# Two transformer blocks in split fp32r: the order of the three products per weight unit when the tokens are stationary

## The chip, the cores and the metric

The kernel runs on one core of one Trainium2 chip, as one program for the whole network. The metric is device time in microseconds (us) of one execution; three executions of the kernel before gave a median of 2867.14 us (2867.01 to 2867.37). The trace that is read here is of another, profiled execution, which took 2861.25 us.

## The reference

256 tokens of width 1024 go through two stacked blocks of two layers each. In the first block a layer is a hybrid mixer (three kinds of attention), a cross-attention to a memory, and a feed-forward part: a dense SwiGLU in layer 0, a mixture of 8 experts with the best 2 per token in layer 1. In the second block a layer is SwiGLU, another hybrid mixer, SwiGLU. Nearly all work is matrix products of fp32 activations with fp32 weights that are read once:

```python
def swiglu(t, w_gu, w_down):
    a, g = jnp.split(t @ w_gu, 2, axis=-1)
    return (jax.nn.silu(a) * g) @ w_down

def moe_swiglu(h, w_router, w_gu, w_down):
    ...
    gate = jnp.einsum('tk,tke->te', top_w, jax.nn.one_hot(top_idx, N_EXPERTS, ...))
    out = jnp.zeros_like(t)
    for e in range(N_EXPERTS):
        out = out + gate[:, e:e + 1] * swiglu(t, w_gu[e], w_down[e])
```

## The kernel before, in words

A product of two fp32 matrices is made of three products in the fp32r format. Each operand is split into a high part (`hi`, the value cast to fp32r) and a low part (`lo`, what the cast left over), and hi times hi, hi times lo and lo times hi are added up in the same PSUM tile; lo times lo is left out.

Weights come from HBM in units of 512 KB: `load_raw` (L156) starts the DMA into a tile `raw`, and `split_raw` (L162) has the scalar engine (ACT) cast it to `hi` (L167) and the vector engine (DVE) take `lo` = `raw` - `hi` (L169). There are 8 buffers each of `raw`, `hi` and `lo`. A unit is 128 partitions by 1024 columns: two row blocks of 128 weight rows with 512 columns (or four with 256, or one with 1024).

"Tokens stationary" means that a 128 by 128 piece of the split activations is loaded into TensorE and a row block of weights streams past it, 512 columns per matmul. `mm3` (L179) issues the three matmuls of one row block: tokens hi by weights hi (L181), tokens hi by weights lo (L182), tokens lo by weights hi (L183). In a row of the trace the first name behind the arrow is the streamed weight part and the second (T, G or Z) the stationary tile, so "mm<-lo,T" is the product with the low part of the weights, and its LDWEIGHTS row is the load of the stationary part for it. `projs` (L188) calls it for every row block of a projection, `proj_steps` (L208) and `merge` do the same in pieces, `proj_acc` (L257) runs the dense down projections with both halves of the columns and both token halves, and `expert` (L962) the down projection of an expert.

The experts take up the middle of the program, from about 862 to 1652 us. Tokens of an expert are gathered into one set of 128 slots. Its 2816 hidden columns come in five chunks of 512 and one of 256. Of a chunk `projs` computes the a half and then the g half, four units each (here a0 to a3 and g0 to g3). Six matmuls a unit make 48 matmuls. When a is complete, ACT takes its tanh (L975), and DVE multiplies it on (L802). When g is complete, DVE multiplies again (L803), four transposes on TensorE (L296, tile `pT`) turn the result, ACT casts it (L285) and DVE takes its low part (L286). After the six chunks two down projections of 11 units each follow, whose result is split (L285 and L286, tile `y`) and scattered back (L1015).

Each engine runs its instructions in a fixed order that is set when the program is built. The order is found by a scheduler of the framework that goes by its own estimates of when operands are ready; the cast and the low part of a unit get a priority 30 places ahead of their turn (`high_priority(offset=self.lead)`), and a low part may be held behind a chain of norm operations (`behind_chain`). So a change in the order of the matmuls can change where, on ACT and DVE, the casts and low parts of units stand against L975, L802, L803 and L286.

The few lines that matter most:

```python
def mm3(self, ps, a, b, first, last):                 # L179, before
    mm(ps, a[0], b[0], start=first, stop=False)       # L181 tokens hi, weights hi
    mm(ps, a[0], b[1], start=False, stop=False)       # L182 tokens hi, weights lo
    mm(ps, a[1], b[0], start=False, stop=last)        # L183 tokens lo, weights hi
```

Of the kernel before, what the change touches and what calls it, by code (L numbers as in the profile page):

```python
# [20 lines left out]
P = 128  # L21
D = 1024
S = 256
KC = D // P
DEPTH = 2
DFF = 2816
FC = DFF // P
# [32 lines left out]
class _Net:  # L60
# [48 lines left out]
    def mm(self):  # L109
        return self.pmm.tile([P, 512], F32, tag="mm", name="mm")  # L110
# [61 lines left out]
    def behind_chain(self):  # L172
# [3 lines left out]
        self.ahead += 1  # L176
        return self.tc.issue_after(self.chain[0 if self.ahead <= self.upto else -1][1])

    def mm3(self, ps, a, b, first, last):  # L179
        mm = self.nc.tensor.matmul  # L180
        mm(ps, a[0], b[0], start=first, stop=False)  # L181
        mm(ps, a[0], b[1], start=False, stop=False)  # L182
        mm(ps, a[1], b[0], start=False, stop=last)  # L183
# [4 lines left out]
    def projs(self, X, jobs, toks=2):  # L188

        work = []  # L190
        self.upto = AHEAD * len(jobs)
        for W, pieces, evac in jobs:
            n = sum(b - a for a, b in pieces)
            per = 2 if n > 256 else 4
            work.append((n, per, evac, [
                self.unit(*[W[k * P:(k + per) * P, a:b].rearrange("(k p) n -> p k n", p=P) for a, b in pieces])
                for k in range(0, KC, per)]))
        self.upto = AHEAD
        for t in range(toks):
            for n, per, evac, units in work:  # L200
                ps = self.mm()[:, :n]
                for k in range(KC):
                    u = units[k // per]
                    self.mm3(ps, (X[0][:, k, t * P:(t + 1) * P], X[1][:, k, t * P:(t + 1) * P]),
                             (u[0][:, k % per], u[1][:, k % per]), k == 0, k == KC - 1)
                evac(t, ps)

    def proj_steps(self, X, W, c0, evac):  # L208

        units = []  # L210

        def step(t):
            if t == 0:
                units.extend(self.unit(W[k * P:(k + 2) * P, c0:c0 + 512].rearrange("(k p) n -> p k n", p=P))
                             for k in range(0, KC, 2))
            ps = self.mm()
            for k in range(KC):
                u = units[k // 2]
                self.mm3(ps, (X[0][:, k, t * P:(t + 1) * P], X[1][:, k, t * P:(t + 1) * P]),
                         (u[0][:, k % 2], u[1][:, k % 2]), k == 0, k == KC - 1)  # L220
            evac(t, ps)
        return [lambda: step(0), lambda: step(1)]

# [33 lines left out]
    def proj_acc(self, lhs, W, kc, fin):  # L257
        tail = min(TAIL, kc)
        self.chain, self.ahead = [], 0
        both = self.ps_s()  # L260
        acc = [[both[:, 0], both[:, 1]], [self.mm(), self.mm()]]

        def step(u, k, t):
            a = lhs(k, t)
            for half in range(2):
                cs = slice(half * 512, (half + 1) * 512)
                self.mm3(acc[t][half], a, (u[0][:, 0, cs], u[1][:, 0, cs]), k == 0, k == kc - 1)

        def get(k):
            return self.unit(W[k * P:(k + 1) * P].rearrange("(k p) n -> p k n", p=P))  # L270

        for k in range(kc - tail):
            u = get(k)
            for t in range(2):
                step(u, k, t)
        us = [get(k) for k in range(kc - tail, kc)]
        for t in range(2):
            for j, u in enumerate(us):
                step(u, kc - tail + j, t)
            fin(t, acc[t])  # L280
# [431 lines left out]
    def merge(self, Y, branches, gates):  # L712

        nc = self.nc
        self.lead = LEAD
        M = self.new_x()
        for c in range(2):
            cs = slice(512 * c, 512 * c + 512)
            units = [[self.unit(w[k * P:(k + 2) * P, cs].rearrange("(k p) n -> p k n", p=P))
                      for k in range(0, w.shape[0] // P, 2)] for _, w, _ in branches]  # L720
            for t in range(2):
                tok = slice(t * P, (t + 1) * P)
                m = None
                for us, (gi, w, k0) in zip(units, branches):
                    ps = self.mm()
                    n = 2 * len(us)
                    for k in range(n):
                        u = us[k // 2]
                        self.mm3(ps, (Y[0][:, k0 + k, tok], Y[1][:, k0 + k, tok]), (u[0][:, k % 2], u[1][:, k % 2]),
                                 k == 0, k == n - 1)  # L730
                    x = self.ptile()[:, :512]
                    nc.vector.scalar_tensor_tensor(x, gates[:, t, gi * D + 512 * c:gi * D + 512 * c + 512], 1.0, ps,
                                                   ALU.add, ALU.mult)
                    if m is not None:
                        nc.vector.tensor_add(x, x, m)
                    m = x
                sl = (slice(None), slice(4 * c, 4 * c + 4), tok)
                self.transpose_split([m[:, j * P:(j + 1) * P] for j in range(4)], M[0][sl], M[1][sl], 0.5)
        return M
# [222 lines left out]
    def expert(self, e, X, back, gate, mids, more, rows):  # L962
# [3 lines left out]
        hi, lo = (a[:, o:o + FC * P].rearrange("p (k s) -> p k s", k=FC) for a in mids)  # L966
        wgu = d["moe_w_gu"][0, e]
        wd = d["moe_w_down"][0, e]
        for c0, c1 in FF_CHUNKS:
            n = c1 - c0  # L970
# [19 lines left out]
        for hf in range(2):  # L990
            cs = slice(hf * 512, (hf + 1) * 512)
            ps = self.mm()
            for k in range(0, FC, 2):
                u = self.unit(wd[k * P:(k + 2) * P, cs].rearrange("(k p) n -> p k n", p=P))
                for j in range(2):
                    self.mm3(ps, (hi[:, k + j], lo[:, k + j]), (u[0][:, j], u[1][:, j]), k + j == 0, k + j == FC - 1)
            if rows and hf:
                rows = rows()
            sums = self.scatter(e, hf, ps, y, back, gate, hf and rows, sums if hf else None)
# [489 lines left out]
```

## Time and profile before

| what | value |
|---|---|
| median of three runs | 2867.14 us (2867.01 to 2867.37) |
| the profiled execution | 2861.25 us, its span in the trace 2859.5 us |
[...]
| TensorE (PE) busy with matmuls | 2785.7 us, 97% |
| loads of stationary parts (PEld) | 2295.5 us, 80% |
| DVE busy | 2186.8 us, 76% |
| ACT busy | 1653.3 us, 58% |
| moved by DMA | 632.97 MB, 221 GB/s in the mean |

How to read it: all engines work at once, each on its own list of instructions, and an instruction waits for its operands with everything behind it on that engine. A busy PE is no PE at its peak, since a matmul's row also covers time in which the next one already streams; what counts is how far apart the matmuls start. In rows of the timeline, "x3" joins three instructions that follow one another, and the brackets give the idle time ahead of a row and what ended it. Waits of an engine that has time to spare cost nothing by themselves.

### The profile page before, as it was taken

The page shows a single profiled execution, that of the slowest core. Times are in us where ns is not written, and L with a number is a line of the kernel's source. Part 1 is how long each engine was busy: PE and PEld are TensorE (multiplying, and loading weights), DVE is VectorE, ACT ScalarE, POOL GpSimd, SP SyncE. Part 2 cuts the span into 40 slices and gives each one's busy share as a digit, 9 for nine tenths or more (in the row PEclk, how much of TensorE's full clock was granted, in tenths as well). Part 3 has the DMA queues.
Part 4 walks back from the last instruction along what each step waited for, and adds up shares of the span by engine and source line. Part 5 has one row for each costly group of instructions (what it writes and reads, how often), then busy time and mean ns, then how long its engine had stood idle before and what let it go on. Part 6 is the DMA issues. An engine that isn't in the chain of part 4 may idle for free.

```text
span 2859.5 us, 39765 instructions
## 1 busy us (share of the span) xinstructions
PE 2785.7 (97%) x14147; PEld 2295.5 (80%) x14147; DVE 2186.8 (76%) x3635; ACT 1653.3 (58%) x2372; POOL 74.0 (3%) x134
## 2 busy tenths in 40 slices
PE   7999999999979999999999989999999999999999
PEld 6779888877967887788778768877788888777887
DVE  7766675777658899999989987597787575887774
ACT  5544454555447677777777756455455454555553
POOL 0100000010000000000000000001000000010000
PEclk9999999999989999999999989999999999999999
DMA  8546466554638999999999976555466566454563
GB/s 268 153 147 206 142 206 190 179 156 137 207 96 311 333 330 359 351 337 361 347 339 356 357 234 191 153 185 161 150 214 193 166 206 192 154 162 154 185 190 99
DMA packets 385583, 632.97 MB, mean 221 GB/s; under 512 B 33888, under 2 KB 171872, under 8 KB 385376
## 3 DMA queue, kind: packets, MB, share of 16 engines
q1 hardware_dynamic: 385376, 630.35, 67.3%
q8 instruction: 113, 1.85, 0.3%
q14 instruction: 94, 0.77, 0.1%
HBM read 629.22 MB, written 1.05 MB: 220 GB/s over the span
## 4 chain that ended last, share of the span: by engine, by line
PE 60%; DVE 7%; issue 1%; ACT 1%; DMA 0%; SPq 0%; ACTq 0%
PE mm L182 13%; PE mm L181 12%; PE mm L183 12%; PE mm L252 9%; PE mm L253 5%; DVE lo L169 2%; PE pS L182 2%; PE pS L181 2%; PE pS L183 2%; PE pT L296 2%; DVE sm L319 0%; PE pT L950 0%; DVE Z L1251 0%; DVE sm L1250 0%; DVE p L1115 0%
## 5 line engine op out<-in xcount | busy, mean ns | idle before, releaser
L169 DVE TENSOR_TENSOR lo<-raw,hi 128x1024 fp32r<-128x1024 f32 (+2 forms) x1170 | 1394.1, 1218 | 312.1 <-ACT hi L167 304.1
L167 ACT CAST hi<-raw 128x1024 fp32r<-128x1024 f32 (+2 forms) x1170 | 1189.6, 1048 | 416.1 <-PE mm L183 260.4
L182 PE MATMUL mm<-lo,T 128*128 128x512 f32 (+3 forms) x1868 | 728.8, 390 | 3.3 <-DVE sm L339 1.8
L181 PE MATMUL mm<-hi,T 128*128 128x512 f32 (+3 forms) x1868 | 719.9, 386 | 8.0 <-PEq L914 5.1
L183 PE MATMUL mm<-hi,T 128*128 128x512 f32 (+3 forms) x1868 | 715.4, 383 | 0.0
L252 PE MATMUL mm<-T,hi 128*128 128x512 f32 x1440 | 500.0, 393 | 0.0
L182 PEld LDWEIGHTS mm<-lo,T 128*128 128x128 f32 x1868 | 353.5, 189 | 90.8 <-DVE lo L169 28.7
L181 PEld LDWEIGHTS mm<-hi,T 128*128 128x128 f32 x1868 | 353.5, 189 | 82.9 <-issue 7.3
L183 PEld LDWEIGHTS mm<-hi,T 128*128 128x128 f32 x1868 | 353.7, 189 | 61.3 <-issue 1.4
L253 PE MATMUL mm<-T,lo 128*128 128x256 f32 x1440 | 400.8, 278 | 0.0
L252 PEld LDWEIGHTS mm<-T,hi 128*128 128x128 f32 x1440 | 269.7, 187 | 61.0
L253 PEld LDWEIGHTS mm<-T,lo 128*128 128x128 f32 x1440 | 271.1, 188 | 0.2
L182 PE MATMUL mm<-lo,G 128*128 128x512 f32 x636 | 249.1, 392 | 0.0
L181 PE MATMUL mm<-hi,G 128*128 128x512 f32 x636 | 248.2, 390 | 0.0
L183 PE MATMUL mm<-hi,Z 128*128 128x512 f32 x572 | 223.4, 390 | 0.0
L182 PEld LDWEIGHTS mm<-lo,G 128*128 128x128 f32 x636 | 119.4, 188 | 25.9 <-DVE lo L169 2.1
L429 POOL TENSOR_SCALAR p<-p,sm 128x256 f32<-128x256 f32 (+1 forms) x128 | 73.3, 585 | 2541.2 <-DVE sm L404 1662.7
L181 PEld LDWEIGHTS mm<-hi,G 128*128 128x128 f32 x636 | 119.5, 188 | 24.4
L183 PEld LDWEIGHTS mm<-hi,Z 128*128 128x128 f32 x572 | 107.4, 188 | 21.6
L285 ACT CAST T<-pT 128x512 fp32r<-128x512 f32 (+3 forms) x112 | 58.0, 521 | 103.3 <-PE pT L296 48.3
L286 DVE TENSOR_TENSOR T<-pT,T 128x512 fp32r<-128x512 f32 (+3 forms) x112 | 67.1, 608 | 50.3 <-ACT T L285 49.8
L254 ACT COPY q<-mm 128x256 f32<-128x256 f32 x180 | 65.6, 364 | 66.3 <-PE mm L253 66.3
(291 smaller groups left out, 2871.7 us busy)
## 6 DMA issues: line engine op xcount, KB each, us to landing
raw<-in_moe_w_gu_dram SPq DMA_DIRECT2D x352, 512.0 KB, 5.4
raw<-in_moe_w_down_dram SPq DMA_DIRECT2D x176, 512.0 KB, 5.8
raw<-in_w_in_dram SPq DMA_DIRECT2D x164, 512.0 KB, 4.5
raw<-in_ffn_w_down_dram SPq DMA_DIRECT2D x110, 512.0 KB, 4.1
raw<-in_ffn_w_gate_dram SPq DMA_DIRECT2D x88, 512.0 KB, 4.6
raw<-in_ffn_w_up_dram SPq DMA_DIRECT2D x88, 512.0 KB, 4.7
raw<-in_ffn_w_gu_dram SPq DMA_DIRECT2D x44, 512.0 KB, 4.7
raw<-in_w_out_dram SPq DMA_DIRECT2D x32, 512.0 KB, 4.1
```

Of the source, the lines that this page charges most:

```text
L167: nc.scalar.copy(hi, raw)
L169: nc.vector.tensor_sub(lo, raw, hi.bitcast(F32))
L181: mm(ps, a[0], b[0], start=first, stop=False)
L182: mm(ps, a[0], b[1], start=False, stop=False)
L183: mm(ps, a[1], b[0], start=False, stop=last)
L252: mm(ps, u[0][:, kk, cs], X[2][:, :, k], start=k == 0, stop=False)
L253: mm(ps[:, 0], u[1][:, kk, cs], X[0][:, k], start=False, stop=k == KC - 1)
L254: nc.scalar.copy(low[:, j], ps[:, 1])
L285: a = nc.scalar.copy(hi, ps)
L286: b = nc.vector.tensor_sub(lo, ps, hi.bitcast(F32))
L296: self.nc.tensor.transpose(ps[:, j * P:(j + 1) * P], s, self.ident)
L429: self.nc.gpsimd.tensor_scalar(dst[:, s], dst[:, s], rc[:, t:t + 1], 1.0, ALU.mult, ALU.mult)
```

## The change

A new helper `mm3x` takes all row blocks of one unit at once. It issues, for each row block, tokens hi by weights hi and tokens lo by weights hi, and after these, for each row block, tokens hi by weights lo. It replaces `mm3` in `projs`, `proj_steps`, the merge of the mixer and the down projection of an expert; in `proj_acc`, whose unit is one row block with two column halves, the same order is written out over the halves. The places where the weights are stationary (`proj_t`, `proj_f`), the router, the mixer's small products and the overflow path stay as they are. Every engine has as many instructions as before.

```diff
--- before.py
+++ after.py
@@ -176,6 +176,16 @@
         self.ahead += 1
         return self.tc.issue_after(self.chain[0 if self.ahead <= self.upto else -1][1])
 
+    def mm3x(self, ps, xs, ws, first, last):
+
+
+        mm = self.nc.tensor.matmul
+        for i, (x, w) in enumerate(zip(xs, ws)):
+            mm(ps, x[0], w[0], start=first and i == 0, stop=False)
+            mm(ps, x[1], w[0], start=False, stop=False)
+        for i, (x, w) in enumerate(zip(xs, ws)):
+            mm(ps, x[0], w[1], start=False, stop=last and i + 1 == len(xs))
+
     def mm3(self, ps, a, b, first, last):
         mm = self.nc.tensor.matmul
         mm(ps, a[0], b[0], start=first, stop=False)
@@ -199,10 +209,10 @@
         for t in range(toks):
             for n, per, evac, units in work:
                 ps = self.mm()[:, :n]
-                for k in range(KC):
-                    u = units[k // per]
-                    self.mm3(ps, (X[0][:, k, t * P:(t + 1) * P], X[1][:, k, t * P:(t + 1) * P]),
-                             (u[0][:, k % per], u[1][:, k % per]), k == 0, k == KC - 1)
+                tok = slice(t * P, (t + 1) * P)
+                for k, u in zip(range(0, KC, per), units):
+                    self.mm3x(ps, [(X[0][:, j, tok], X[1][:, j, tok]) for j in range(k, k + per)],
+                              [(u[0][:, j], u[1][:, j]) for j in range(per)], k == 0, k + per == KC)
                 evac(t, ps)
 
     def proj_steps(self, X, W, c0, evac):
@@ -214,10 +224,10 @@
                 units.extend(self.unit(W[k * P:(k + 2) * P, c0:c0 + 512].rearrange("(k p) n -> p k n", p=P))
                              for k in range(0, KC, 2))
             ps = self.mm()
-            for k in range(KC):
-                u = units[k // 2]
-                self.mm3(ps, (X[0][:, k, t * P:(t + 1) * P], X[1][:, k, t * P:(t + 1) * P]),
-                         (u[0][:, k % 2], u[1][:, k % 2]), k == 0, k == KC - 1)
+            tok = slice(t * P, (t + 1) * P)
+            for k, u in zip(range(0, KC, 2), units):
+                self.mm3x(ps, [(X[0][:, j, tok], X[1][:, j, tok]) for j in (k, k + 1)],
+                          [(u[0][:, j], u[1][:, j]) for j in range(2)], k == 0, k + 2 == KC)
             evac(t, ps)
         return [lambda: step(0), lambda: step(1)]
 
@@ -262,9 +272,13 @@
 
         def step(u, k, t):
             a = lhs(k, t)
-            for half in range(2):
-                cs = slice(half * 512, (half + 1) * 512)
-                self.mm3(acc[t][half], a, (u[0][:, 0, cs], u[1][:, 0, cs]), k == 0, k == kc - 1)
+            mm = self.nc.tensor.matmul
+            cuts = list(zip(acc[t], (slice(0, 512), slice(512, D))))
+            for ps, cs in cuts:
+                mm(ps, a[0], u[0][:, 0, cs], start=k == 0, stop=False)
+                mm(ps, a[1], u[0][:, 0, cs], start=False, stop=False)
+            for ps, cs in cuts:
+                mm(ps, a[0], u[1][:, 0, cs], start=False, stop=k == kc - 1)
 
         def get(k):
             return self.unit(W[k * P:(k + 1) * P].rearrange("(k p) n -> p k n", p=P))
@@ -724,10 +738,9 @@
                 for us, (gi, w, k0) in zip(units, branches):
                     ps = self.mm()
                     n = 2 * len(us)
-                    for k in range(n):
-                        u = us[k // 2]
-                        self.mm3(ps, (Y[0][:, k0 + k, tok], Y[1][:, k0 + k, tok]), (u[0][:, k % 2], u[1][:, k % 2]),
-                                 k == 0, k == n - 1)
+                    for k, u in zip(range(0, n, 2), us):
+                        self.mm3x(ps, [(Y[0][:, k0 + j, tok], Y[1][:, k0 + j, tok]) for j in (k, k + 1)],
+                                  [(u[0][:, j], u[1][:, j]) for j in range(2)], k == 0, k + 2 == n)
                     x = self.ptile()[:, :512]
                     nc.vector.scalar_tensor_tensor(x, gates[:, t, gi * D + 512 * c:gi * D + 512 * c + 512], 1.0, ps,
                                                    ALU.add, ALU.mult)
@@ -992,8 +1005,8 @@
             ps = self.mm()
             for k in range(0, FC, 2):
                 u = self.unit(wd[k * P:(k + 2) * P, cs].rearrange("(k p) n -> p k n", p=P))
-                for j in range(2):
-                    self.mm3(ps, (hi[:, k + j], lo[:, k + j]), (u[0][:, j], u[1][:, j]), k + j == 0, k + j == FC - 1)
+                self.mm3x(ps, [(hi[:, j], lo[:, j]) for j in (k, k + 1)], [(u[0][:, j], u[1][:, j]) for j in range(2)],
+                          k == 0, k + 2 == FC)
             if rows and hf:
                 rows = rows()
             sums = self.scatter(e, hf, ps, y, back, gate, hf and rows, sums if hf else None)
```

The build finds new places for some casts and low parts. Line numbers after the change are 13 or 14 higher: L802 is L815, L803 is L816, L975 is L988, L286 is L300, L343 is L357, and L184, L185, L187 are hi by hi, tokens lo by weights hi, and weights lo.

The first place is the second chunk of the third expert on DVE; its tanh is the L975 at 1076.71 us in the trace before. Here mm_21404 is the a half of a chunk, mm_21455 its g half; lo_21401 belongs to a3, lo_21434, 21440, 21446 and 21452 to g0 to g3, and lo_21493 to a0 of the next chunk. Before:

```order
L286 TENSOR_TENSOR Z_7985<-pT_21373,G_7984 128x512
L169 TENSOR_TENSOR lo_21401<-raw_21398,hi_21400 128x1024
L169 TENSOR_TENSOR lo_21434<-raw_21431,hi_21433 128x1024
L169 TENSOR_TENSOR lo_21440<-raw_21437,hi_21439 128x1024
L802 SCALAR_TENSOR_TENSOR p_21429<-p_21429,mm_21404 128x512
L169 TENSOR_TENSOR lo_21446<-raw_21443,hi_21445 128x1024
L169 TENSOR_TENSOR lo_21452<-raw_21449,hi_21451 128x1024
L169 TENSOR_TENSOR lo_21493<-raw_21490,hi_21492 128x1024
L803 SCALAR_TENSOR_TENSOR p_21480<-p_21429,mm_21455 128x512
```

After, on the same engine and at the same place:

```order
L300 TENSOR_TENSOR Z_7985<-pT_21373,G_7984 128x512
L169 TENSOR_TENSOR lo_21401<-raw_21398,hi_21400 128x1024
L169 TENSOR_TENSOR lo_21434<-raw_21431,hi_21433 128x1024
L815 SCALAR_TENSOR_TENSOR p_21429<-p_21429,mm_21404 128x512
L169 TENSOR_TENSOR lo_21440<-raw_21437,hi_21439 128x1024
L169 TENSOR_TENSOR lo_21446<-raw_21443,hi_21445 128x1024
L169 TENSOR_TENSOR lo_21452<-raw_21449,hi_21451 128x1024
L169 TENSOR_TENSOR lo_21493<-raw_21490,hi_21492 128x1024
L816 SCALAR_TENSOR_TENSOR p_21480<-p_21429,mm_21455 128x512
```

The multiplication by the a half (L802, now L815) has moved one low part earlier, so that the low part of g1 stands behind it. The same holds for 27 of the 40 chunks of 512 columns: the second to fifth chunk of experts 2, 4 and 6 (counted from 0), and all five of experts 3, 5 and 7.

On ACT at the same place, before:

```order
L285 CAST G_7984<-pT_21373 128x512
L167 CAST hi_21400<-raw_21398 128x1024
L167 CAST hi_21433<-raw_21431 128x1024
L167 CAST hi_21439<-raw_21437 128x1024
L975 ACTIVATE p_21429<-mm_21404 128x512
L167 CAST hi_21445<-raw_21443 128x1024
```

And after:

```order
L299 CAST G_7984<-pT_21373 128x512
L167 CAST hi_21400<-raw_21398 128x1024
L167 CAST hi_21433<-raw_21431 128x1024
L988 ACTIVATE p_21429<-mm_21404 128x512
L167 CAST hi_21439<-raw_21437 128x1024
L167 CAST hi_21445<-raw_21443 128x1024
```

The tanh (L975, now L988) has moved ahead of the cast of g1 in the same way. On PE the four transposes of a chunk's result come after a1's first matmul, where they came after four of a0's six.

The third place is the start of the dense feed-forward part of the first layer on DVE, at about 341 us: p_3297 and p_3324 are the first token half's products (L802 and L803), the sm tiles belong to the norm of the second token half, and h_88 is its result. Before:

```order
L802 SCALAR_TENSOR_TENSOR p_3297<-p_3297,mm_3272 128x512
L319 SCALAR_TENSOR_TENSOR sm_3189<-sm_3190,sm_3189 128x1
L315 SCALAR_TENSOR_TENSOR sm_3190<-sm_3189,sm_3191 128x1
L319 SCALAR_TENSOR_TENSOR sm_3189<-sm_3190,sm_3189 128x1
L315 SCALAR_TENSOR_TENSOR sm_3190<-sm_3189,sm_3191 128x1
L319 SCALAR_TENSOR_TENSOR sm_3189<-sm_3190,sm_3189 128x1
L343 SCALAR_TENSOR_TENSOR h_88<-h_88,sm_3189,gb_2978 128x512 x2
L803 SCALAR_TENSOR_TENSOR p_3324<-p_3297,mm_3299 128x512
```

After:

```order
L815 SCALAR_TENSOR_TENSOR p_3297<-p_3297,mm_3272 128x512
L329 SCALAR_TENSOR_TENSOR sm_3190<-sm_3189,sm_3191 128x1
L333 SCALAR_TENSOR_TENSOR sm_3189<-sm_3190,sm_3189 128x1
L329 SCALAR_TENSOR_TENSOR sm_3190<-sm_3189,sm_3191 128x1
L816 SCALAR_TENSOR_TENSOR p_3324<-p_3297,mm_3299 128x512
L333 SCALAR_TENSOR_TENSOR sm_3189<-sm_3190,sm_3189 128x1
L329 SCALAR_TENSOR_TENSOR sm_3190<-sm_3189,sm_3191 128x1
L333 SCALAR_TENSOR_TENSOR sm_3189<-sm_3190,sm_3189 128x1
L357 SCALAR_TENSOR_TENSOR h_88<-h_88,sm_3189,gb_2978 128x512 x2
```

The second product (L803, now L816) has moved ahead of the last steps of the norm of the second token half.

## Rows read from the trace of the kernel before

**Rows 1.** The page: busy times, and loads of stationary parts by line.

```profile
PE 2785.7 (97%) x14147; PEld 2295.5 (80%) x14147; DVE 2186.8 (76%) x3635; ACT 1653.3 (58%) x2372; POOL 74.0 (3%) x134
...
L182 PEld LDWEIGHTS mm<-lo,T 128*128 128x128 f32 x1868 | 353.5, 189 | 90.8 <-DVE lo L169 28.7
L181 PEld LDWEIGHTS mm<-hi,T 128*128 128x128 f32 x1868 | 353.5, 189 | 82.9 <-issue 7.3
```

**Rows 2.** Timeline of PE and its loader (PEld), one chunk of expert 2.

```profile
1071.25 0.42 PEld L296 LDWEIGHTS pT<-ident,p 128*128 128x128 f32 x4 [0.30 <-DVE p L803]
1073.64 0.39 PE L181 MATMUL mm<-hi,T 128*128 128x512 f32 x1
1073.87 0.39 PE L182 MATMUL mm<-lo,T 128*128 128x512 f32 x1
1074.09 0.39 PE L183 MATMUL mm<-hi,T 128*128 128x512 f32 x1
1076.28 0.40 PE L183 MATMUL mm<-hi,T 128*128 128x512 f32 x1
1079.56 0.19 PEld L182 LDWEIGHTS mm<-lo,T 128*128 128x128 f32 x1 [0.35 <-DVE lo L169]
1081.96 0.39 PE L183 MATMUL mm<-hi,T 128*128 128x512 f32 x1
```

**Rows 3.** Waits of the loader for low parts, 862 to 1652, then after 1652.

```profile
PEld mm L182 <- DVE lo L169: 27.3, 96, 0.4
...
PEld mm L182 <- DVE lo L169: 2.3, 1, 2.3
```

**Rows 4.** Start of the dense part in layer 0, loader and DVE.

```profile
337.56 0.19 PEld L182 LDWEIGHTS mm<-lo,T 128*128 128x128 f32 x1 [1.20 <-DVE lo L169]
343.76 0.42 PEld L296 LDWEIGHTS pT<-ident,h 128*128 128x128 f32 x4 [1.11 <-PE mm L183]
342.89 1.42 DVE L343 SCALAR_TENSOR_TENSOR h<-h,sm,gb 128x512 f32<-128x512 f32 x2
```

**Rows 5.** Stretches: PE, PEld, DVE, ACT, POOL busy (x); clock, DMA share, GB/s.

```profile
1017.20:1216.60 199.40, 199.40 (x938) 159.67 (x938) 183.92 (x197) 144.57 (x165) 0.00 (x0) 1.00 0.99 348
870.00:915.50 45.50, 45.50 (x210) 37.21 (x209) 44.48 (x45) 37.15 (x41) 0.00 (x0) 1.00 1.00 352
1124.00:1157.00 33.00, 33.00 (x148) 26.86 (x147) 29.77 (x32) 23.61 (x26) 0.00 (x0) 1.00 1.02 365
```

**Rows 6.** Timeline of DVE, the same chunk (x2, x3: joined rows).

```profile
1070.51 0.69 DVE L803 SCALAR_TENSOR_TENSOR p<-p,mm 128x512 f32<-128x512 f32 x1 [0.65 <-PE mm L183]
1071.11 2.36 DVE L169 TENSOR_TENSOR lo<-raw,hi 128x1024 fp32r<-128x1024 f32 x2
1073.38 0.69 DVE L286 TENSOR_TENSOR Z<-pT,G 128x512 fp32r<-128x512 f32 x1
1073.98 3.49 DVE L169 TENSOR_TENSOR lo<-raw,hi 128x1024 fp32r<-128x1024 f32 x3
1077.39 0.68 DVE L802 SCALAR_TENSOR_TENSOR p<-p,mm 128x512 f32<-128x512 f32 x1
1078.28 3.50 DVE L169 TENSOR_TENSOR lo<-raw,hi 128x1024 fp32r<-128x1024 f32 x3 [0.22 <-ACT hi L167]
1082.39 0.69 DVE L803 SCALAR_TENSOR_TENSOR p<-p,mm 128x512 f32<-128x512 f32 x1 [0.61 <-PE mm L183]
```

**Rows 7.** Timeline of ACT in expert 0.

```profile
888.07 1.05 ACT L167 CAST hi<-raw 128x1024 fp32r<-128x1024 f32 x1 [0.30 <-PE mm L183]
892.67 0.60 ACT L975 ACTIVATE p<-mm 128x512 f32<-128x512 f32 x1 [0.30 <-PE mm L183]
904.06 0.60 ACT L975 ACTIVATE p<-mm 128x512 f32<-128x512 f32 x1 [0.30 <-PE mm L183]
```

**Rows 8.** Timeline of ACT, the same chunk.

```profile
1076.71 0.60 ACT L975 ACTIVATE p<-mm 128x512 f32<-128x512 f32 x1 [1.34 <-PE mm L183]
1077.21 4.83 ACT L167 CAST hi<-raw 128x1024 fp32r<-128x1024 f32 x5
```

## The prediction, made before the changed kernel had run

> **What bounds the kernel now.** The page comes first: PE is busy for 97% of the span [rows 1], so the question is how far apart its matmuls start, and where it stands still. On the timeline the reader is to see that matmuls of 512 columns start 0.23 us apart (1073.64, 1073.87, 1074.09), whether the next one keeps the stationary part (L181 to L182) or changes it (L182 to L183) [rows 2]. Then the view of the waits: the only waits that the edit is aimed at are those of the loader for a low part, and they sum to 27.3 us in 96 places among the experts, one of 2.3 us behind them [rows 3] and one of 1.20 us ahead of them [rows 4]. The experts are therefore where the time is decided.
>
> There DVE is busy for 183.9 of 199.4 us and the DMA share is 0.99 [rows 5], so three resources are nearly full at once. The timeline of one chunk tells which ends last. From one L803 to the next it takes 1082.39 - 1070.51 = 11.88 us [rows 6]. Expert 0, where the casts wait for PE to free a buffer and so are far ahead, takes 904.06 - 892.67 = 11.39 us for the same chunk [rows 7]. That is PE's own floor: 48 matmuls at some 0.2265 us are 10.87, and the four transposes take 0.5. A later chunk thus loses 0.49 us. It loses it in a loop through all engines: a's last matmul starts at 1076.28 [rows 2], the tanh follows 0.43 us later at 1076.71 [rows 8], L802 at 1077.39, the low part of g2 behind it at 1078.28 to 1079.50 [rows 6], the loader gets it at 1079.56 after a wait of 0.35, g's last matmul starts at 1081.96 [rows 2], and L803 follows 0.43 later. DVE's rows of that chunk sum to 2.36 + 0.69 + 3.49 + 0.68 + 3.50 + 0.69 = 11.41 us [rows 6], so DVE can't make up for a wait.
>
> **The change part by part.** *The matmuls themselves.* Each engine has as many instructions as before. In the new order the stationary part changes at every matmul; as it costs 0.23 us either way [rows 2], I take 0.
>
> [...] The loader makes 1868 loads for L182, as many as for L181, though both use the same stationary part [rows 1]. [...]
>
> *Low parts are met later.* Of a unit's six matmuls the first to need the low part was the second and is now the fifth: 3 x 0.2265 = 0.68 us later. That is more than the longest ordinary wait of 0.4 [rows 3]. The transposes also come three matmuls later, so their wait of 0.30 for L803 goes [rows 2]. If nothing else moved, a chunk of 11.88 us would fall to the floor of some 11.44 (0.05 kept for joints), 0.44 us less.
>
> *The tanh and L802 move.* This does not stay alone: in 27 chunks L802 and the tanh now stand ahead of the low part and the cast of g1, where they stood ahead of those of g2. Both must wait for the end of a, and with them now one unit more. I set the start of the tanh to 0 and lay the rows behind it. The first cast behind it starts at 0.50 (1077.21 - 1076.71) [rows 8] and takes about 1.03, so hi of g1 is there at 1.53. L802 runs from 0.68 to 1.36 [rows 6]. The low part of g1 starts 0.04 after the cast, as that of g2 did at 1078.28, and takes 1.22: done at 2.79. On PE a's last matmul started at -0.43; g0's six follow, and g1's first would start at -0.43 + 7 x 0.2265 = 1.16. It waits for the cast until about 1.58. Its four high matmuls go by 2.49, then it waits for the low part until 2.85. From there the restart (0.11) and 13 more matmuls set g's last start at 5.90, and L803 at 6.33. Before, this half took 1082.39 - 1076.71 = 5.68, so it is 0.65 longer. The other half, from L803 to the tanh, took 6.20 with its waits; without them 24 matmuls and 0.50 for transposes give 5.94 to 5.99. Together the chunk takes about 12.30 us, 0.42 more than before. The bounds: 0.44 less (nothing of the move is felt) and 0.65 more with nothing won in the first half. I take 0.42, since the same steps give the 11.88 of before from its own order: 27 x 0.42 = +11.3 us.
>
> That what stands behind a waiting product waits too is seen where L803 idles DVE for 0.61 with low parts queued behind it [rows 6]. [...] Could DVE take a low part past a waiting L802, the sum would be that of the first rival below.
>
> *Chunks whose order stays.* The first chunk of experts 2, 4 and 6 keeps its order, and one chunk of expert 1 gets a better one: 4 x -0.44 = -1.8. Expert 0 is at the floor already: 0.
>
> *The down projections of experts 3, 5 and 7.* At six places a low part moves behind the split of y, which waits for the end of the column half. Bounds: 0, and one low part each (6 x 1.14 = 6.8). PE has 11 units without a product between here, and fewer low parts wait; I take 0.25 each, +1.5.
>
> *Outside the experts.* At most the 2.3 and 1.20 us above can be won. At the start of the dense part L803 of the first token half is put ahead of the norm of the second. Before, L343 started at 342.89, while PE reached the transposes at 343.76 [rows 4]. Now L343 waits for L803, thus for the end of g. With the 1.20 won, g ends at about 342.6, L803 runs from 343.0 to 343.7, three small steps take 0.6, and the transposes start 0.87 after L343, at about 345.2: +1.4. With half of the 2.3 won that is about 0. Bounds -4 and +4: casts, low parts and norms change places at the other seams too, and each is worth about one low part (1.14).
>
> The sum is 11.3 - 1.8 + 1.5 + 0 = +11.0 us. On the profiled execution's 2861.25 that is 2872.3 us; it lies 5.9 below the median of the runs, and since the work is the same I add the sum to the median: 2878.1, say 2878.
>
> **The rivals.** *Faster.* The move isn't felt, say because the first units of g stand further ahead than my rows of one chunk say, and all of some 31 chunks reach 11.44: 31 x -0.44 = -13.6, and -3.5 outside: 2850. For it: expert 0 shows the floor, and 8 units of 0.524 MB in 11.44 us need 367 GB/s, near the 365 of a down projection [rows 5]. Against it: L802 needs the whole of a, and stands behind no spare unit.
>
> *No change.* The relief of 0.44 and the later g1 cancel, so that the waits only change their names, or the seams give back what the chunks lose. For it: DMA moves 348 GB/s at a share of 0.99, and expert 0 got 352 [rows 5] while 8 units in 11.39 us need 368, so it was using up a stock; a chunk at 11.88 needs 353. If that is the limit, the relief is worth nothing and the lost time at g1 is partly bought back by fuller buffers. Within 5 us of before: 2867.
>
> *Slower still.* The wait for hi of g1 also delays the casts of a0 and a1, which in turn bring the transposes' cast (L285) late; the loop then loses a full 0.87 a chunk (the 0.42 and what the relief should have won once more): 23.5 us, 2890. It decides if the row of L803 no longer shows a wait for PE.
>
> **How the numbers follow.** Forecast 0.48, own range 2871 to 2885; faster 0.27, no change 0.13, slower still 0.12. Within 0.2% (5.7 us) no measurement of this kernel would tell a difference from none. So slower 0.60, same 0.13, faster 0.27. The range reaches down to the faster rival and up to between forecast and the worst: 2850 to 2889.
>
> **What would show it.** In the profile after: the period of L803 in experts 2 to 7 at about 12.3 us (11.4 if the faster rival holds); waits of PE or its loader for the cast (hi L167, about 0.4) and then the low part (about 0.35) of g1 in each chunk, and none for low parts in the a half; no wait of the transposes for L803; L802 waiting about 0.9 us on DVE; DMA below 348 GB/s between 1017 and 1216. The prediction is wrong if the waits for g1 are missing, or if the stretch of the experts keeps its 199.4 us a pair.

## The result, and the profile after

The changed kernel took 2885.44 us in the median of four runs (2883.1 to 2890.18), against 2867.07 (2863.7 to 2867.37) for the kernel before beside it. The ratio is 1.0069 with a 95% interval of 1.0057 to 1.0081: slower by about 20 us. The forecast was 2878 with a range of 2850 to 2889, and the sign came from the mechanism it named. The forecast change was 11 us; some 8 us more lie at places where the forecast had put 0.

The first view is the timeline of DVE after the change, in a chunk that is ordered as in the pieces ahead of the prediction (L815 is the L802 of before, L816 the L803, L300 the L286). It answers to [rows 6]; this is the third chunk of expert 2.

```profile
1091.34 0.69 DVE L816 SCALAR_TENSOR_TENSOR p<-p,mm 128x512 f32<-128x512 f32 x1 [0.18 <-PE mm L187]
1091.94 2.35 DVE L169 TENSOR_TENSOR lo<-raw,hi 128x1024 fp32r<-128x1024 f32 x2
1094.21 0.69 DVE L300 TENSOR_TENSOR Z<-pT,G 128x512 fp32r<-128x512 f32 x1
1094.93 2.36 DVE L169 TENSOR_TENSOR lo<-raw,hi 128x1024 fp32r<-128x1024 f32 x2
1097.88 0.69 DVE L815 SCALAR_TENSOR_TENSOR p<-p,mm 128x512 f32<-128x512 f32 x1 [0.58 <-ACT p L988]
1098.81 4.63 DVE L169 TENSOR_TENSOR lo<-raw,hi 128x1024 fp32r<-128x1024 f32 x4 [0.25 <-ACT hi L167]
1103.62 0.69 DVE L816 SCALAR_TENSOR_TENSOR p<-p,mm 128x512 f32<-128x512 f32 x1 [0.18 <-PE mm L187]
```

From L816 to L816 it is 1103.62 - 1091.34 = 12.28 us, where before it was 11.88. L815 stands two low parts behind L300 instead of three, so DVE gets to it 0.58 us before the tanh is done, and idles. The four low parts behind it (the first of them is g1's) are late with it. On ACT, which answers to [rows 8], the cast that now stands behind the tanh starts 0.50 us after it:

```profile
1097.24 0.60 ACT L988 ACTIVATE p<-mm 128x512 f32<-128x512 f32 x1 [1.40 <-PE mm L187]
1097.74 5.78 ACT L167 CAST hi<-raw 128x1024 fp32r<-128x1024 f32 x6
```

On PE and its loader, which answer to [rows 2], both waits that the forecast named stand where it put them, first for the cast of g1 and then for its low part:

```profile
1098.83 0.19 PEld L184 LDWEIGHTS mm<-hi,T 128*128 128x128 f32 x1 [0.69 <-ACT hi L167]
1100.09 0.30 PEld L187 LDWEIGHTS mm<-lo,T 128*128 128x128 f32 x2 [0.50 <-DVE lo L169]
```

Over all experts the waits of the loader answer to [rows 3]: 96 short waits for low parts became 27 for casts, one for each chunk that the build had moved, and 39 for low parts.

```profile
PEld mm L187 <- DVE lo L169: 18.5, 39, 0.5
PEld mm L184 <- ACT hi L167: 18.0, 27, 0.7
```

The page says nearly nothing of it. Busy times are the same, and one sees only that the span grew (columns: busy us, share, instructions):

```profile
PE 2795.5 (97%) x14147; PEld 2306.1 (80%) x14147; DVE 2189.8 (76%) x3635; ACT 1650.0 (57%) x2372; POOL 77.2 (3%) x134
```

To see where the time went I laid the starts of the same matmuls (counted by their place in PE's order; both traces have 14147) and tanhs of both traces beside each other. The profiled execution of the changed kernel took 2887.31 us, 26.06 more than that of before, more than the medians differ. How far it lags at some places of the program (times of before):

| place | lag, us |
|---|---|
| 62 us, in the first mixer | 3.6 |
| 230, behind that mixer | 6.3 |
| 360, dense part under way | 7.6 |
| 680, behind the second mixer | 10.2 |
| first tanh of expert 0 (869.92) | 10.04 |
| last tanh of expert 7 (1617.96) | 19.86 |
| 1700, second block under way | 22.6 |
| 1790, behind its first gate and up projections | 24.4 |
| end | 26.0 |

The experts add 9.8 us, the rest 16 in this execution. Two of the signs that the forecast named are here as well: a pair of experts takes 203.0 us in place of 199.4 (first tanh of expert 2 to that of expert 4), and DMA moves 344 GB/s from 1025.7 to 1226.4 us, where [rows 5] has 348.

### The profile page after: what moved, and what is told of

Its sections match the earlier page's. It is cut to its first block, busy times and chain, and to the rows that moved or that the text cites. A ratio compares the mean times of both kernels' runs of the same rounds, so it can differ in the third digit from the quotient of the medians.

```text
span 2885.5 us, 39820 instructions
## 1 busy us (share of the span) xinstructions
PE 2795.5 (97%) x14147; PEld 2306.1 (80%) x14147; DVE 2189.8 (76%) x3635; ACT 1650.0 (57%) x2372; POOL 77.2 (3%) x134
## 4 chain that ended last, share of the span: by engine, by line
PE 58%; DVE 8%; issue 2%; ACT 2%; DMA 1%; ACTq 0%; DVEq 0%; SPq 0%
PE mm L187 11%; PE mm L184 10%; PE mm L185 10%; PE mm L262 9%; PE mm L263 5%; DVE lo L169 3%; PE pS L278 2%; PE pS L281 2%; PE pS L279 2%; PE pT L310 1%; PE mm L278 1%; PE mm L279 1%; PE mm L281 1%; ACT hi L167 1%; PE pS L437 0%
## 5 line engine op out<-in xcount | busy, mean ns | idle before, releaser
L184 PE MATMUL mm<-hi,T 128*128 128x512 f32 (+3 forms) x1760 | 679.4, 390 | 15.8 <-ACT hi L167 6.3
L185 PE MATMUL mm<-hi,T 128*128 128x512 f32 (+3 forms) x1760 | 673.3, 385 | 0.0
L187 PE MATMUL mm<-lo,T 128*128 128x512 f32 (+3 forms) x1760 | 530.7, 385 | 1.8
L184 PEld LDWEIGHTS mm<-hi,T 128*128 128x128 f32 x1760 | 333.9, 190 | 97.1 <-ACT hi L167 18.6
L185 PEld LDWEIGHTS mm<-hi,T 128*128 128x128 f32 x1760 | 334.6, 190 | 62.0 <-issue 2.1
L187 PEld LDWEIGHTS mm<-lo,T 128*128 128x128 f32 x1760 | 320.1, 189 | 75.0 <-DVE lo L169 15.9
L184 PE MATMUL mm<-hi,G 128*128 128x512 f32 x416 | 162.7, 391 | 0.0
L185 PE MATMUL mm<-hi,Z 128*128 128x512 f32 x352 | 137.4, 390 | 0.0
L187 PE MATMUL mm<-lo,G 128*128 128x512 f32 x416 | 129.9, 393 | 0.3
L300 DVE TENSOR_TENSOR T<-pT,T 128x512 fp32r<-128x512 f32 (+3 forms) x112 | 67.1, 607 | 56.1 <-ACT T L299 55.9
L299 ACT CAST G<-pT 128x512 fp32r<-128x512 f32 x66 | 37.0, 561 | 97.7 <-PE pT L310 97.6
L187 PEld LDWEIGHTS mm<-lo,G 128*128 128x128 f32 x416 | 77.3, 188 | 19.0 <-DVE lo L169 3.3
L184 PEld LDWEIGHTS mm<-hi,G 128*128 128x128 f32 x416 | 78.1, 188 | 15.8
```

Of the source, the lines that this page charges most:

```text
L184: mm(ps, x[0], w[0], start=first and i == 0, stop=False)
L185: mm(ps, x[1], w[0], start=False, stop=False)
L187: mm(ps, x[0], w[1], start=False, stop=last and i + 1 == len(xs))
L299: a = nc.scalar.copy(hi, ps)
```

## The experiments

Each kernel ran on one chip beside the kernel before; ratios are to it, and 0.1% is 2.9 us. A lag is, as above, how much later the same place in PE's order is reached than in the trace of before.

**Which half of the program.** Two kernels apply the new order on one side only. `mm3x` gets a switch, set around the call of `expert`; in the first, `proj_acc` also keeps its old step.

```diff
 def mm3x(self, ps, xs, ws, first, last):
     mm = self.nc.tensor.matmul
+    if self.old:
+        for i, (x, w) in enumerate(zip(xs, ws)):
+            self.mm3(ps, x, w, first and i == 0, last and i + 1 == len(xs))
+        return
...
+            was, self.old = self.old, False        # True in the second kernel
             self.expert(e, ...)
+            self.old = was
```

> The new order only in the experts (their gate, up and down projections); everywhere else the old order. DVE's order in the experts is then that of the changed kernel. Theory 1 (the time is lost in the chunks, where the tanh and L802 stand one unit earlier): the change's 10.9 us between the first tanh of expert 0 and the transition behind expert 7 stay, with a period of 12.27 us a chunk, and nothing outside: 2867 + 11 = 2878. Rival (the loss outside the experts belongs to the change as much): this run keeps only about half of the change's 18 to 20 us. Rival 2 (the loss outside is run-to-run scatter, the whole change is the chunks): this run measures the same as the whole change, 2885.

Measured: ratio 1.0037 (1.0023 to 1.0051), some 10.6 us slower. The chunks take 12.27 us as in the whole change. Theory 1 holds for this half, but not all of it is the chunks: in its trace 9.9 us come between the first tanh of expert 0 and the last of expert 7, and 1.8 more at the seam behind the experts, of which more below.

> The new order everywhere but in the experts, whose order on DVE and ACT is then that of before. Theory 1: the experts go back to 11.88 us a chunk and the 10.9 us are gone; what is left is the loss outside, which the profile put at about 9 us ahead of the experts and 4 behind them: 2867 + 8 to 13 = 2875 to 2880. Rival (what the profile showed outside is scatter): 2867, no change.

Measured: 1.0029 (1.0019 to 1.0039), some 8.3 us slower, with the experts' chunks back at 11.88 to 11.95, as before. So the loss outside is no scatter. The two halves add up to 18.9 us, which is the whole within its interval (16 to 23 us).

**The place of the tanh.** If the loss in the experts comes from the place and not from the order of the products, putting the tanh and its product back must turn it into a gain. To have something to stand behind, the units of both halves of a chunk are asked for together, and the two instructions are held, in issue order alone, behind the cast and the low part of g1.

```diff
-            self.proj(X, wgu, [(c0, c1)], on_a, toks=1)
-            self.proj(X, wgu, [(DFF + c0, DFF + c1)], on_g, toks=1)
+            self.projs(X, [(wgu, [(c0, c1)], on_a), (wgu, [(DFF + c0, DFF + c1)], on_g)], toks=1)
...
+                self.hold = self.splits[-4 + 1] if e > 0 and n == 512 else None   # g1: (cast, low part)
+                with self.behind(0):                                             # issue_after(cast)
                     nc.scalar.activation(th, ps, AF.Tanh, scale=0.5)
...
+        with self.behind(1):                                                     # issue_after(low part)
             nc.vector.scalar_tensor_tensor(th, th, 1.0, pa, ALU.add, ALU.mult)
```

> The changed kernel, with the tanh and the product by it (L802 before) of experts 1 to 7 held on their engines behind the cast and the low part of g1, where they stood before the change; for this the units of a chunk's a and g halves are asked for together, which also moves one low part at some ends of an expert. Theory 1: without the moved places the later use of low parts is a gain, as in the first chunks of experts 2, 4 and 6, which kept their place and took 11.34 us: 27 chunks fall from 12.27 to 11.35, 25 us less than the changed kernel: 2860. Rival (the hold moves the wait to a0 of the next chunk, and the period goes to 11.9): 2875.

Measured: 2859.26 us, ratio 0.9989 (0.998 to 0.9998). The chunks fell to 11.35 us, but for the first of experts 3, 5 and 7 with 11.70 to 11.77, where the asking together changed the end of the expert ahead. Theory 1 holds: the same products in the same order are some 23 us faster (ratio 0.9989 in place of 1.0069) with two instructions moved by one place.

> The new order only in the experts, with the same hold behind g1 and a and g asked for together; the old order outside. Theory 1: 30 chunks of 11.88 fall to 11.35, 16 us less than before: 2851, faster than both kernels. Rival (the reading of the loop is wrong and the hold costs a wait elsewhere): 2867 or above.

Measured: 2850.52 us, ratio 0.9953 (0.994 to 0.9967): 13.5 us faster than the kernel before, and the fastest of all. On DVE in this kernel L822 is the product by the tanh and L824 the next one:

```profile
1097.41 3.50 DVE L171 TENSOR_TENSOR lo<-raw,hi 128x1024 fp32r<-128x1024 f32 x3
1100.82 0.68 DVE L822 SCALAR_TENSOR_TENSOR p<-p,mm 128x512 f32<-128x512 f32 x1
1101.42 3.49 DVE L171 TENSOR_TENSOR lo<-raw,hi 128x1024 fp32r<-128x1024 f32 x3
1105.16 0.69 DVE L824 SCALAR_TENSOR_TENSOR p<-p,mm 128x512 f32<-128x512 f32 x1 [0.26 <-PE mm L197]
```

Three low parts ahead of it again, and neither L822 nor the low parts behind it wait. The tanhs of this stretch show the period, 1111.07 - 1099.72 = 11.35 us, against 11.39 for expert 0 in [rows 7]:

```profile
1099.72 0.60 ACT L1000 ACTIVATE p<-mm 128x512 f32<-128x512 f32 x1 [0.44 <-PE mm L197]
...
1111.07 0.60 ACT L1000 ACTIVATE p<-mm 128x512 f32<-128x512 f32 x1 [0.44 <-PE mm L197]
```

This also speaks against the limit that the rival *No change* had named, a DMA that gives no more than about 350 GB/s. In the chunks of expert 2 of this kernel it moved 373 (columns as in [rows 5]):

```profile
1078.00:1124.00 46.00, 46.00 (x236) 39.12 (x235) 44.77 (x47) 35.31 (x41) 0.00 (x0) 1.00 1.04 373
```

The other half of the edit, asking for both halves together with nothing held, was tried by itself:

> The changed kernel with only the other half of the held runs' edit: the units of a and g of a chunk are asked for together, and nothing is held. The tanh and the product by it stay one unit early, as the change put them. If the hold is what brought the gain, the chunks stay at 12.27 us and the run at 2880 to 2887, as the changed kernel. Rival (asking together brings the gain by itself): chunks at 11.35, 2860.

Measured: 2884.93 us, 1.0069 (1.0052 to 1.0086), with chunks of 12.27 us. The hold made the gain.

**Is the new order needed for the gain?** The old order of the products with the tanh and its product held one unit later than they stood before. The diff is that of the hold, with `- 4 + 2` and `self.old` set throughout.

> The old order everywhere, with the tanh and its product in experts 1 to 7 held one unit later than before, behind the cast and low part of g2, as they stand in expert 0; a and g are asked for together. Theory 1 (what counts is how many low parts DVE has ahead when the tanh comes; the order of the products only shifts when they are needed): a chunk falls from 11.88 to 11.4 us without any new order, 31 x 0.48 = 15 us: 2849 to 2853 on the scale of the runs before at 2864. Rival (only the later use of the low parts brings the gain): the chunk stays at 11.88 or grows, 2864 or above, since L802 later makes g's result later.

Measured: 2858.03 us, 0.9976 (0.9965 to 0.9986), 6.9 us faster, with chunks of 11.65 us. Neither the theory's 11.4 nor the rival's 11.88. L803 of before is L824 here:

```profile
1095.63 0.69 DVE L824 SCALAR_TENSOR_TENSOR p<-p,mm 128x512 f32<-128x512 f32 x1 [0.69 <-PE mm L203]
...
1107.29 0.69 DVE L824 SCALAR_TENSOR_TENSOR p<-p,mm 128x512 f32<-128x512 f32 x1 [0.69 <-PE mm L203]
```

The waits for low parts in the second half of the chunk went, but those in the first half stay, since there the low parts of a1 and a2 are needed early by the old order:

```profile
1096.37 0.42 PEld L316 LDWEIGHTS pT<-ident,p 128*128 128x128 f32 x4 [0.30 <-DVE p L824]
1097.51 0.19 PEld L202 LDWEIGHTS mm<-lo,T 128*128 128x128 f32 x1 [0.21 <-DVE lo L171]
1100.37 0.19 PEld L202 LDWEIGHTS mm<-lo,T 128*128 128x128 f32 x1 [0.28 <-DVE lo L171]
```

So both count. The four combinations, all measured in experts 2 to 7:

| order of the products | low parts of g issued ahead of the product by the tanh | chunk, us |
|---|---|---|
| old | g0, g1 (kernel before) | 11.88 |
| old | g0, g1, g2 | 11.65 |
| new | g0 (changed kernel) | 12.27 |
| new | g0, g1 | 11.35 |

The table is for experts 2 to 7, where DVE makes eight low parts a chunk, as many as PE uses. In expert 1 of the kernel before the old order took 11.35 us as well (L803 at 981.62 and at 992.97), though L802 waits there as L815 does after the change:

```profile
985.22 2.36 DVE L169 TENSOR_TENSOR lo<-raw,hi 128x1024 fp32r<-128x1024 f32 x2
988.16 0.69 DVE L802 SCALAR_TENSOR_TENSOR p<-p,mm 128x512 f32<-128x512 f32 x1 [0.58 <-ACT p L975]
989.09 3.49 DVE L169 TENSOR_TENSOR lo<-raw,hi 128x1024 fp32r<-128x1024 f32 x3 [0.25 <-ACT hi L167]
```

DVE makes only seven low parts in that chunk (two more stand at 982.22), so it lives on a lead of units, and the last chunk of this expert takes 11.87 us. By these rows DVE's wait of 0.58 us for the tanh costs nothing by itself; it costs when the low part behind it is the next that PE needs, as in the changed kernel with its 12.27 us.

**The loss outside the experts.** Two kernels split it by helper, with the experts in the old order: the new step only in `proj_acc`, and the new order only in the projections, gate steps and merge.

> The new order only in proj_acc (the dense down projections and the output projections), the old order elsewhere. All but the experts cost 8.0 us. Theory A (the norm behind a projection starts later): in the new order the first column half's last matmul is the last but one of the projection, three matmuls later in relation to the second half than before, so the norm's first step on DVE, and with it the transposes, start up to 0.45 us later at each of some ten seams; this run then costs 4 to 5 of the 8 us. Theory B (the projections behind the norm finish sooner and only wait longer for the norm, then run at half clock): proj_acc alone costs under 1 us.

Measured: 1.0020 (1.0011 to 1.0029), some 5.7 us.

> The new order outside the experts in the projections, the gate steps and the merge, but not in proj_acc; the experts keep the old order. Theory A: 3 to 4 us of the 8 are left. Theory B: 7 to 8 us are left, and the profile shows the half-clock stretches behind the seams (near 540 and 1695 us) that the run with all but the experts shows.

Measured: 1.0018 (1.0009 to 1.0027), some 5.2 us. Together they are 10.9 where the run with all but the experts lost 8.3; the intervals overlap. Neither theory holds alone, and both pieces cost.

The half-clock stretch near 1695 that theory B named appears with the projections (mean clock 0.68 from 1690.11 to 1699.40) and not with `proj_acc`. But it appears as well with the new order in the experts alone (mean 0.80 from 1694.97 to 1703.47), where all behind the experts is in the old order, so it isn't the projections' own. The one near 540 appears with neither alone: there PE's loader stands still for 2.12 us with `proj_acc`, 2.39 with the projections, and 2.58 with both, and with both the clock falls in all five traces (in the changed kernel to 0.50, from 538.25 to 541.50).

In the trace of `proj_acc` lags grow near 105 (by 1.7 us between 90 and 130), near 345 (1.9) and near 600 (1.2). The last two sit at seams where a norm follows, but that the later end of the first column half is their cause was not tried by itself. That near 105 is not the edit's: the trace of the kernel with the old order throughout and the tanh held loses 1.8 us there, behind the same wait of 1.53 us, and the clock falls in both (means of 0.71 and 0.70 in the stretches below), as it does not in the trace of before (1.00 from 104 to 110). First `proj_acc`, then the old order:

```profile
105.00:110.79 5.79, 5.79 (x24) 3.57 (x24) 2.47 (x9) 1.47 (x5) 0.00 (x0) 0.71 0.69 193
```

```profile
104.24:109.99 5.75, 5.75 (x23) 3.75 (x23) 2.46 (x9) 1.47 (x5) 0.00 (x0) 0.70 0.71 204
```

One seam was tried by itself. The place of L803 at the start of the dense part was put back in the kernel with all but the experts:

```diff
+        with self.tc.issue_after(self.normed) if first else nullcontext():   # last step of the norm
             nc.vector.scalar_tensor_tensor(s, th, 0.5, pg, ALU.mult, ALU.mult)
```

> As the run with all but the experts, but with L803 of the first token half at the start of the dense part held behind the last step of the norm of the second half, as it stood before. One look at the profile. Theory (the place of L803 costs the 1.5 us that this seam lost): the drift against the kernel before between 330 and 360 us falls from 1.5 to 1.7 us to about 0.3. Rival (the norm itself is late, since PE waited 2.57 us for it there): the drift stays above 1.2.

Measured: between 330 and 360 us the lag fell by 0.3 us, where it grew by 1.4 without the hold. In this one execution the number is the theory's, the cause only in part. Without the hold L821 (L803 before) waits for PE and the norm's L362 comes behind it:

```profile
345.05 0.69 DVE L821 SCALAR_TENSOR_TENSOR p<-p,mm 128x512 f32<-128x512 f32 x1 [0.16 <-PE mm L192]
...
346.29 1.41 DVE L362 SCALAR_TENSOR_TENSOR h<-h,sm,gb 128x512 f32<-128x512 f32 x2
```

With it, the norm (L363) goes first:

```profile
348.40 1.42 DVE L363 SCALAR_TENSOR_TENSOR h<-h,sm,gb 128x512 f32<-128x512 f32 x2
349.74 0.68 DVE L823 SCALAR_TENSOR_TENSOR p<-p,mm 128x512 f32<-128x512 f32 x1
```

That makes the transposes 0.70 us earlier: the loader stands 1.87 us ahead of them instead of 2.57. The other 1.1 us is the clock. Behind the 2.57 it was 0.58 (from 347.19 to 350.01) in the kernel with all but the experts, behind the 1.87 it was 1.00. And it does not always fall behind the 2.57. The kernel that asks for a and g together has the same instructions at this seam as the changed kernel; the clock fell in the one and not in the other. First the changed kernel, the load behind the gap and the stretch that follows:

```profile
350.36 1.57 PEld L310 LDWEIGHTS pT<-ident,h 128*128 128x128 f32 x8 [2.57 <-issue]
```

```profile
350.39:353.59 3.20, 3.20 (x12) 2.64 (x13) 1.81 (x3) 1.17 (x2) 0.00 (x0) 0.50 1.06 360
```

Then the kernel that asks for a and g together:

```profile
346.49 0.42 PEld L315 LDWEIGHTS pT<-ident,h 128*128 128x128 f32 x4 [2.57 <-issue]
```

```profile
346.52:348.82 2.30, 2.25 (x12) 1.38 (x13) 1.53 (x3) 1.17 (x2) 0.00 (x0) 1.00 0.98 340
```

At a clock of 0.50 twelve matmuls take 3.20 us, at 1.00 they take 2.30. The seam lost 1.4 us in the first and 0.4 in the second.

The run as a whole took 2874.39 us in its single execution, from which no difference of 2 us can be read.

## Why the prediction was right, and which step failed

*The matmuls themselves: 0.* Right. In the changed kernel's undisturbed chunks, as in the held ones, 48 matmuls and four transposes take 11.35 us.

*Low parts are met later: 0.44 us won where nothing moves.* Right, a little low: the first chunks of experts 2, 4 and 6 kept their place and took 11.35 us, where they had taken 11.91 to 11.95. In experts 2 to 7 the old order, with the tanh one unit later, stops at 11.65.

*The tanh and L802 move: +0.42 in 27 chunks.* Right: 12.27 to 12.28 in place of 11.88, and 27 waits for a cast. From the tanh at 1097.24 to L816 at 1103.62 it is 6.38 us, for the 6.33 forecast; the other half, from L816 at 1091.34 to the tanh, takes 5.90, for 5.94 to 5.99. The single waits are off: the loader waits 0.69 and 0.50 us where about 0.4 and 0.35 were forecast, and L815 0.58 where it was 0.9.

*The down projections of experts 3, 5 and 7: +1.5.* Not borne out there. From the tanh of the last, narrow chunk to the first tanh of the next expert, the ends of experts 3 and 5 went from 44.88 to 44.59 us, while those of 2, 4 and 6 took 0.3 us more. At expert 7 the lag grew by 0.35 in the down projection and by 0.9 until the next transposes.

*The experts' sum: +11.0.* Measured 9.8 in the traces. The 10.6 of the run with the experts alone holds the loss at the seam behind them as well. Expert 1 gave 1.2 us back instead of 0.44. So the sum is right, the chunks' part in its steps too, while its small terms were off in both directions.

*The norm behind L803 at the dense part: +1.4.* Right in its size by luck. The forecast had the transposes at 345.2 instead of 343.76, 1.44 later. The changed kernel lags by 6.24 us ahead of this seam and has them at 350.36, so they are 0.36 later: L816, forecast at 343.0, starts at 348.25, which is 342.0 without the lag. The rest of the loss is the clock behind the stand of 2.57 us (0.50 from 350.39 to 353.59), for which the forecast has no term, and which two other executions with the same stand don't show.

*Outside the experts: about 0, from -4 to +4.* This step failed. It measured +8.3 (0.19 to 0.39%). The forecast counted the waits for low parts of 2.3 and 1.20 us as time to be won, and put the clock at nothing. The seam behind the experts shows why that was wrong. Before, after PE's wait for a low part, the transposes of the second token half waited 0.59 us for the norm:

```profile
1669.33 0.29 PEld L182 LDWEIGHTS mm<-lo,T 128*128 128x128 f32 x1 [2.27 <-DVE lo L169]
1683.09 0.42 PEld L296 LDWEIGHTS pT<-ident,p 128*128 128x128 f32 x4 [0.59 <-issue]
```

In the kernel with all but the experts the low part is in time, and PE waits for the norm 4.42 us instead, at the same place (the trace there lags by 10.0 us):

```profile
1693.06 1.57 PEld L315 LDWEIGHTS pT<-ident,p 128*128 128x128 f32 x8 [4.42 <-issue]
```

What ended last there was the norm's chain on DVE. Its last step starts 0.87 us ahead of the transposes before, and 0.86 with all but the experts:

```profile
1682.22 1.41 DVE L372 SCALAR_TENSOR_TENSOR p<-h,sm,rows 128x512 f32<-128x512 f32 x2
```

```profile
1692.20 1.41 DVE L391 SCALAR_TENSOR_TENSOR p<-h,sm,rows 128x512 f32<-128x512 f32 x2
```

From the first token half's transposes to those of the second it is 18.35 us before and 18.34 with all but the experts, so nothing was won. Worse, the granted clock fell at the longer gap. Views of stretches, first before and then with all but the experts (columns as in [rows 5]):

```profile
1676.00:1684.00 8.00, 7.77 (x37) 6.08 (x36) 6.84 (x19) 2.49 (x7) 0.00 (x0) 1.00 1.05 345
1684.00:1690.00 6.00, 5.98 (x30) 4.80 (x29) 4.52 (x7) 3.79 (x6) 0.00 (x0) 1.00 0.49 150
```

```profile
1686.00:1693.00 7.00, 3.06 (x14) 2.21 (x12) 5.83 (x18) 2.29 (x6) 0.00 (x0) 0.97 1.05 347
1693.00:1700.00 7.00, 6.91 (x23) 5.69 (x24) 4.55 (x7) 2.81 (x4) 0.00 (x0) 0.55 0.56 178
```

Behind the gap of 4.42 us the clock is 0.55 in the mean of the stretch, behind that of 0.59 before it is 1.00; 23 matmuls start in 7 us where 30 started in 6, and this seam loses some 2.3 us. The chance of 0.60 for slower rested on the chunks alone, and the chunks alone would have borne it out.

What stays open: of the 8 us outside, the dense seam (1.4 us in the trace with all but the experts, 0.4 where the clock held) and the seam behind the experts (some 2.3) are explained by rows. The lags in the two mixers (some 6 us in that trace) go with both pieces of the edit, and their single causes weren't separated; 1.0 of them, near 105, goes with a fall of the clock that untouched kernels show too. How much of the 8 us is the clock and how much are norms that come later is not shown.

## What to carry to other kernels

When a scheduler sets the order, an edit on one engine must be read on the others too: here the order of six matmuls was worth 0.5 us a chunk and the place of two small instructions 0.9, with opposite signs, and the sign of the whole came from the second. Count how many operands an engine has issued ahead when it meets an instruction that waits for the consumer (here DVE stood for 0.58 us at L815, with four low parts behind it), and hold it there by an explicit order. A wait taken away in front of another engine's chain was no gain here (18.34 us for 18.35 at the seam behind the experts); see what is late next, and what the clock is behind the longer gap (0.55 there, for 1.00). And before a lag in one trace is put down to an edit, look for it at the same place in the trace of a kernel that the edit left alone there.

## What the runs showed of the hardware that was not expected

Stretches at a granted clock of 0.50 appear behind gaps of the matrix engine of 1.42 to 4.62 us, and not each time behind the same gap. At four seams, in the eleven traces of this case (the gap is the loader's idle time ahead of the transposes there, "fell" means that a stretch at 0.50 follows, and "full" that the clock stays at 1.00):

| seam | gap, us | granted clock behind it |
|---|---|---|
| near 105 | 1.42 to 1.53 | fell in 7 traces, full in 4; the kernels with the old order at this place are on both sides |
| near 345 | 1.09 to 1.87 | full in 5 |
| near 345 | 2.12 | fell in 1 |
| near 345 | 2.57 | fell in 3, full in 2 |
| near 535 | 1.04 to 2.39 | full in 6 |
| near 535 | 2.58 to 2.59 | fell in 5 |
| behind the experts | 0.59 to 1.90 | full in 3 |
| behind the experts | 3.64 to 4.62 | fell in 8 |

A gap of 2.12 us was followed by a fall at one seam (near 345) and by the full clock at another (near 535), in the same trace (with `proj_acc` alone). What decides it is not shown here.

The unchanged gate and up projections of the second block, in which a matmul of 512 columns and one of 256 alternate, ran at either of two speeds in different executions at a granted clock of 1.00. In 90 us of the same stretch the kernel before starts 521 matmuls, the changed kernel 511; the kernel with the experts alone starts 521 there, but lags by the same 1.9 us in two other such projections. First before, then after, then the experts alone:

```profile
1700.00:1790.00 90.00, 90.00 (x521) 79.38 (x520) 67.25 (x90) 53.51 (x81) 0.00 (x0) 1.00 0.66 195
```

```profile
1723.00:1813.00 90.00, 90.00 (x511) 78.08 (x510) 66.01 (x86) 52.38 (x79) 0.00 (x0) 1.00 0.64 192
```

```profile
1713.50:1803.50 90.00, 90.00 (x521) 79.34 (x520) 67.25 (x89) 53.58 (x81) 0.00 (x0) 1.00 0.65 196
```

At 1.7 to 1.9 us a projection this is likely part of the scatter of 3 to 7 us between executions of one kernel, as is the clock near 105; what sets the speed was not tried. Both make single profiles of this kernel lag in places that the edit never touched.
